# Expert blocks of a mixture of experts: weights as the resting operand in the first two products

## The chip, the cores and the metric

The kernel runs on one core of a Trainium2 chip. The metric is the device time of one execution in microseconds (us). TensorE multiplies matrices: a resting operand of up to 128 x 128 is loaded (LDWEIGHTS, PEld in the profile), and up to 512 columns of a moving operand stream through it (MATMUL, PE). Results land in banks of PSUM, of 128 partitions x 512 float32. VectorE (DVE), ScalarE (ACT) and GpSimd (POOL) work on tiles in SBUF, DVE and ACT also in PSUM; SyncE (SP) issues most transfers.

## What is computed

One layer: an mLSTM mixer, a norm, a mixture of experts, a second norm and a gated embedding, for 1024 tokens of 1024 elements. The change is in the mixture of experts. Each token goes to two of 16 experts:

```python
for e in range(N_EXPERTS):
    h = jax.nn.silu(t @ w_gate[e]) * (t @ w_up[e])
    y = y + gate[:, e:e + 1] * (h @ w_down[e]).astype(jnp.float32)
```

`w_gate` and `w_up` are 1024 x 512 and `w_down` is 512 x 1024 in float32. The kernel computes only the tokens that were routed to an expert.

## The kernel before, in words

To keep float32 accuracy at TensorE's faster rate, each operand is split in a high part (a rounded copy, made by ScalarE) and a low part (the rest, made by VectorE or GpSimd). A product is three matmuls: high x high, high x low, low x high (`product`, line 60, and `split`, line 56).

The experts are worked through in 16 steps, r = 0 to 15. They are ranked by their number of tokens, and `ORDER` (line 42) takes ranks 0, 8, 1, 9 and so on: even r are the eight experts of ranks 0 to 7, odd r the others. Every expert has a first block of 128 tokens. Those of ranks 0 to 7 have a second block of 64 (`mini`, line 716). Tokens beyond these go to a loop at the end that runs as often as the routing asks (line 1461).

For a step r the order is: rows of tokens are gathered (`locate`, 739) and transposed by TensorE (`turn`, 746; `turn_mini`, 750); the gate product; a silu; the up product; their product h; the transposes of h; the down product. In gate and up products the transposed tokens rest and 512 columns of the weights stream. `first_full` (600) does this for 128 tokens: one bank, eight steps of three matmuls. `first_mini` (626) does it for the second block: the 64 high parts and the 64 low parts of its tokens rest side by side, so two matmuls a step do, and `fold` (658) adds the two halves of the bank. h comes out with tokens on partitions and is transposed (`tr_full`, 581, with 128 tokens; `tr_mini`, 592, with 64) for `full_out` (672) and `mini_out` (687).

The main loop (1353) interleaves: while expert r's up and down products run, the gate product of r + 1 stands between them, and the transposes of the tokens of r + 2 stand among the steps of the down product of r (line 1423). The transposes of h of an odd r stand behind the gate product of 128 tokens of r + 1 (line 1400) and ahead of its `first_mini` (1404). Those of an even r stand after four steps of the next gate product (1388).

Weights come in pieces of 1 MB, six to an expert, through four raw buffers (line 486), and each piece is split in two chunks of 1024 columns. The splits wait in a queue (`queue_piece`, 513) and `tick` (542) takes one out after every second step of products; GpSimd makes the low part of every fourth piece. In this stage the order of TensorE, ScalarE, VectorE and GpSimd is the order of the program text (`manual_schedule`, 971 to 976); SyncE's is set by a planner.

PSUM has four banks for products (`pmm`, 491) and three for transposes (`ptr`, 405).

Of the kernel before, what the change touches and what calls it, by code (L numbers as in the profile page):

```python
# [13 lines left out]
F32 = mybir.dt.float32  # L14
# [10 lines left out]
D = 1024  # L25
# [20 lines left out]
def trunk(ctx, tc, io, out):  # L46
# [77 lines left out]
    # ------------------------------------------------ token mixer  # L124
    pw = ExitStack()
    with ExitStack() as pa:
# [34 lines left out]
        def first_load():  # L161
            """the first units' weights and columns of x, in the order of their use"""
# [18 lines left out]
        def qk_units(*us, first=False, between=lambda: None):  # L181
            """the convolved queries or keys of heads; between is traced after half of the products"""
# [75 lines left out]
        def gates():  # L258
            """the gates' running sums and maxima, in two steps"""
# [142 lines left out]
        # output projection's weights and first rows, beside the last of the input projection  # L402
# [62 lines left out]
        def mixed(t, p):  # L465
            """a tile's gated heads and their parts, in steps; the last leaves the transposes"""
# [26 lines left out]
    # ------------------------------------------------ experts' parts  # L493
# [10 lines left out]
    def new_piece(kind):  # L504
        """kind: 0 and 1 for the first products' weights, 2 for the second's"""
# [7 lines left out]
    def queue_piece(raw, shape, kind, eng=None):  # L513
        """a piece whose split is queued, to be traced among the products"""
# [27 lines left out]
    def tick():  # L542
        """after a step of products: every second a queued split, if the clock runs"""
# [6 lines left out]
    def load_part(fetch, m, eng=None, kind=None):  # L550
        """the two pieces of an expert's m-th weights"""
# [9 lines left out]
    def find_tokens(e, parts, nt=NT, p=None, pi=None):  # L561
        """tokens of slots: e [128 tokens, nt, slots] marks a slot's token; parts: ranges of slots"""
# [18 lines left out]
    def tr_full(res, src, nk, name):  # L581
        """[128 tokens, nk * 128] to the parts of its transpose, [128, nk, 128 tokens]"""
        if nk == NF:
            both = mt([128, 2, nk, 128], F32R, name=name)
            res += [both[:, i] for i in range(2)]
        else:
            res += [mt([128, nk, 128], F32R, name=f"{name}{i}") for i in range(2)]
# [22 lines left out]
    def first_halves(res, x, w):  # L610
        """as first_full, the products with the weights' hi parts first, and by halves of the columns"""
# [27 lines left out]
    def part(f, *a):  # L639
        """a list for what a chain makes, and the chain"""  # L640
# [3 lines left out]
    def run(chain, n=NT * NE, also=None, first=0, every=1):  # L644
        """the next n steps of a chain of products, with the steps of another among them"""
# [17 lines left out]
    def silu(g, n):  # L663
        sg = mt([128, DE], F32, name="sg")
# [22 lines left out]
    def mini_out(h, w, dst):  # L687
        yo = mt([128, D], F32, name="yo")
        for n in range(2):
            ps = pmm.tile([128, 512], F32, name="mm")  # L690
            ns = slice(512 * n, 512 * n + 512)
            for k in range(NF):
                wh, wl = use(w[k // 2])
                product(ps, [(h[0][:, k], wh[:, k % 2, ns]), (h[0][:, k], wl[:, k % 2, ns])],
# [21 lines left out]
    mini = lambda i: ORDER[i] < NMINI  # L716

# [11 lines left out]
    def late_fetch(raw, m, half):  # L729
        """a fetch for the second block's expert from the scalar engine's queue"""  # L730
# [3 lines left out]
    def mark(e, v, width):  # L734
        """marks of a position's tokens: e [128 tokens, NT, width]"""
# [3 lines left out]
    def locate(r):  # L739
        """gathers of a block's tokens, by the table's columns"""  # L740
        e = ORDER[r]
        X[r] = gather_x(tab[:, 0, e:e + 1], 128)
        if mini(r):
            XM[r] = gather_x(tab[:, 1, e:e + 1], 64)

    def turn(r):
        rows, X[r] = X[r], []
# [11 lines left out]
    def embed():  # L759
        """rows of the embedding's projection, in steps"""  # L760
# [19 lines left out]
    # ------------------------------------------------ output projection, norm, router  # L780
    pm_, pe_ = ExitStack(), ExitStack()
    with ExitStack() as pb_:
# [10 lines left out]
        # the norm's gain and bias go into the router's weights:  # L793
        # x1 @ rw = (z @ (g rw) - mean sum(g rw)) / std + b @ rw
# [19 lines left out]
        def residual(t):  # L814
            """the residual's rows of a tile"""
# [3 lines left out]
        def project(t, yt):  # L819
            """a tile's output projection in steps"""  # L820
# [17 lines left out]
        def normed(t, n):  # L838
            """half of a tile's sum, its parts and its moments"""
# [49 lines left out]
        def select(c0, c1, new=None):  # L889
            """the experts of tiles c0 to c1: scores and one-hots of the two"""  # L890
# [12 lines left out]
            def places(res, a, m):  # L903
                """of every four in a: how many come before it, larger or as large and to its left"""
# [68 lines left out]
        for t in range(NT - 1):  # L973
# [38 lines left out]
            if t < NT - 2:  # L1012
# [23 lines left out]
             "xgm xt0 xt1 ht sg yo idx idf ohb ef wi svb bs mv")  # L1036
        space = [mt([128, D], F32, name="space", tag=f"xt{i}") for i in range(2)]
# [58 lines left out]
    # ------------------------------------------------ experts  # L1096
    with pe_:
        PIECES[2] = [pe_.enter_context(pool(f"moew{i}", reuse_waits="tile")) for i in range(4, 6)]
        home(pe_.enter_context(pool("moex", reuse_waits="tile")), "xg")
        home(pm_.enter_context(pool("moem", reuse_waits="tile")), "xm hm gs us fold e")  # L1100
# [28 lines left out]
        # what the slots need takes the room of constants that are no longer needed  # L1129
# [7 lines left out]
        key, idr = r1(), r1()  # L1137
# [577 lines left out]
```

## Time and profile before

| | |
|---|---|
| three runs | 1011.25, 1011.89, 1013.51 us |
| median | 1011.89 us |
| span of the profiled execution, first to last instruction | 1008.3 us |
| what lies around that span, against the median | 3.6 us |
| TensorE busy | 973.3 us, 97% |
| VectorE, ScalarE, GpSimd busy | 667.0, 561.8, 302.0 us |
| mean granted clock of TensorE | 0.989 of full speed |

The profile shows one execution. A row of the timeline gives the start and the duration in us, the engine, the line of the kernel, the operation, the tile written and the tiles read, and in brackets the idle time ahead of it with what ended it. A matmul's duration is its way through the pipeline; how fast matmuls follow each other is read from their starts. Line 63 is in `product`, line 57 the high part and 58 the low part of a split, lines 522 and 523 those of a weight piece.

### The profile page before, as it was taken

To read this page: it belongs to the slowest core of one execution; us is meant where nothing else is said; L and a number is where in the kernel's file an instruction comes from. 1 tells how busy PE (TensorE), PEld (TensorE's weight loads), DVE (VectorE), ACT (ScalarE), POOL (GpSimd) and SP (SyncE) were. 2 spreads that over 40 slices of the span, in tenths; PEclk is the share of its full clock that TensorE was granted. 3 is DMA by queue.
4 is the path that set the end of the run, shared out by engine and by line. 5 is a ranking of instruction groups with operands and counts; after the bars stand their busy time and mean duration, and the time that the engine had idled before them with its cause. 6 is when DMAs were issued, how large, how long until landed. Compare 5 with 4: busy or idle time off the path is not lost. (4 is left out here: it accounts for less than half of the span.)

```text
span 1008.3 us, 15211 instructions
## 1 busy us (share of the span) xinstructions
PE 973.3 (97%) x5596; PEld 823.0 (82%) x5596; DVE 667.0 (66%) x1217; ACT 561.8 (56%) x928; POOL 302.0 (30%) x269
## 2 busy tenths in 40 slices
PE   7999999999999999997789999999999999989998
PEld 5989999899999887886467687878787878767887
DVE  6567667461542578879966689866657575577883
ACT  6346546363562455665447666766767676653431
POOL 0002203030100112225647424334252524354442
PEclk9999999999999999999979999999999999999999
DMA  8126811203354364522657998989898988754531
GB/s 320 47 69 266 305 58 59 84 33 93 101 183 155 136 251 150 187 67 117 223 177 289 377 330 290 342 290 335 297 336 298 342 325 296 268 194 149 184 127 63
DMA packets 51396, 207.05 MB, mean 205 GB/s; under 512 B 6892, under 2 KB 15724, under 8 KB 38264
## 3 DMA queue, kind: packets, MB, share of 16 engines
q1 hardware_dynamic: 43720, 182.74, 50.4%
q0 software_dynamic: 5824, 21.50, 6.1%
q10 hardware_dynamic: 1776, 1.81, 0.5%
q8 instruction: 45, 0.74, 0.3%
q14 instruction: 31, 0.25, 0.1%
HBM read 170.35 MB, written 35.68 MB: 204 GB/s over the span
## 5 line engine op out<-in xcount | busy, mean ns | idle before, releaser
L523 POOL TENSOR_TENSOR wlo<-wraw,whi 128x1024 fp32r<-128x1024 f32 x64 | 166.2, 2615 | 223.9 <-ACT whi L522 211.4
L522 ACT ACTIVATE whi<-wraw 128x1024 fp32r<-128x1024 f32 x204 | 205.5, 1051 | 12.9 <-DMA wraw<-eu 4.3
L523 DVE TENSOR_TENSOR wlo<-wraw,whi 128x1024 fp32r<-128x1024 f32 x140 | 172.5, 1259 | 38.8 <-ACT whi L522 37.7
L63 PE MATMUL mm<-whi,xt 128*128 128x512 f32 (+1 forms) x528 | 171.9, 396 | 2.2 <-DVE xt L58 1.5
L63 PE MATMUL mm<-wl,xh 128*128 128x256 f32 (+1 forms) x512 | 145.9, 285 | 0.0
L63 PE MATMUL mm<-wh,xh 128*128 128x256 f32 (+1 forms) x512 | 145.6, 284 | 0.0
L63 PE MATMUL mm<-wh,xl 128*128 128x256 f32 (+1 forms) x512 | 145.4, 284 | 0.0
L63 PEld LDWEIGHTS mm<-whi,xt 128*128 128x128 f32 x528 | 98.6, 191 | 23.7 <-DVE xt L58 2.0
L63 PE MATMUL mm<-wlo,xt 128*128 128x512 f32 (+1 forms) x264 | 100.9, 391 | 4.5 <-DVE wlo L523 4.5
L63 PEld LDWEIGHTS mm<-wh,xh 128*128 128x128 f32 x512 | 97.0, 189 | 0.1
L63 PEld LDWEIGHTS mm<-wl,xh 128*128 128x128 f32 x512 | 96.9, 189 | 0.1
L63 PEld LDWEIGHTS mm<-wh,xl 128*128 128x128 f32 x512 | 96.9, 189 | 0.0
L63 PE MATMUL mm<-woh,yt 128*128 128x512 f32 x256 | 93.6, 412 | 0.0
L63 PE MATMUL mm<-whi,ht 128*128 128x512 f32 x240 | 87.4, 413 | 2.3 <-ACT ht L57 1.4
L63 PE MATMUL mm<-whi,x2t 128*128 128x512 f32 (+1 forms) x272 | 84.7, 386 | 0.4 <-ACT x2t L57 0.4
L63 PEld LDWEIGHTS mm<-wlo,xt 128*128 128x128 f32 x264 | 49.5, 191 | 14.2 <-DVE wlo L523 4.9
L63 PEld LDWEIGHTS mm<-whi,x2t 128*128 128x128 f32 x272 | 50.1, 188 | 11.2 <-ACT x2t L57 0.9
L58 DVE TENSOR_TENSOR wl<-wr,wh 128x1024 fp32r<-128x1024 f32 (+2 forms) x26 | 29.7, 1144 | 44.3 <-ACT wh L57 44.0
L63 PE MATMUL mm<-xh,wh 128*128 128x512 f32 x128 | 50.7, 405 | 7.1 <-ACT xh L57 7.1
L63 PEld LDWEIGHTS mm<-whi,ht 128*128 128x128 f32 x240 | 45.5, 190 | 13.5 <-ACT ht L57 2.0
L63 PEld LDWEIGHTS mm<-woh,yt 128*128 128x128 f32 x256 | 48.1, 188 | 8.8
L63 PE MATMUL mm<-whi,xm 128*128 128x512 f32 x128 | 52.7, 412 | 0.0
(381 smaller groups left out, 2042.2 us busy)
## 6 DMA issues: line engine op xcount, KB each, us to landing
wraw<-eg SPq DMA_DIRECT2D x32, 1024.0 KB, 7.0
wraw<-ed SPq DMA_DIRECT2D x32, 1024.0 KB, 6.3
wraw<-eu SPq DMA_DIRECT2D x31, 1024.0 KB, 6.5
y_d<-zt SPq DMA_DIRECT2D x16, 512.0 KB, 5.6
y_d<-yo SPq DMA_DIRECT2D x14, 512.0 KB, 6.2
num_d<-nb SPq DMA_DIRECT2D x32, 128.0 KB, 1.8
wr<-wo SPq DMA_DIRECT2D x8, 512.0 KB, 4.6
sig_d<-sg SPq DMA_DIRECT2D x32, 128.0 KB, 1.8
```

What stands on the lines that cost most here:

```text
L58: (eng or V).tensor_tensor(lo, src, f32(hi), op=ALU.subtract)
L63: PE.matmul(ps, a, b, start=start and i == 0, stop=stop and i == n - 1)
L522: S.activation(hi[:, c], raw[:, c], AF.Copy)
L523: e.tensor_tensor(lo[:, c], raw[:, c], f32(hi)[:, c], op=ALU.subtract)
```

## The change

For the seven even steps r = 2, 4 ... 14 the gate and up products are turned round: 128 columns of the weights rest, and the tokens of both blocks stream, n = 128 + `extra(r)` of them, high parts and low parts side by side. The weights' high part meets both (2n columns), the low part meets the high parts (n columns). The results have h's columns on partitions, four groups in four banks, so h needs no transposes. `extra` is the size of the second block by rank, 64 for ranks 0 and 1 and 8 fewer for each rank after that. r = 0 stays as it was. The tokens of both blocks are transposed into one tile (`xw`), in four groups instead of two and two, all among the down product of r - 2. Tiles `ht`, `sg`, `xt0` and `xt1` get one buffer instead of two.

```diff
+    def tr_columns(dst, srcs):
+        for src, c0, n in srcs:
+            for q in range(0, ND, 4):
+                turned(src, q, *[dst[:, q:q + 4, i, c0:c0 + n] for i in range(2)], n)
+                yield
+
+    def first_columns(x, w, done):
+        n = x.shape[3]
+        ps = [pmm.tile([128, 512], F32, name="mm") for _ in range(NF)]
+        for half in range(2):
+            for f in range(NF):
+                wh, wl = use(w[half])
+                fs = slice(128 * f, 128 * f + 128)
+                for k in range(4):
+                    xk = x[:, 4 * half + k]
+                    first, end = half + k == 0, half == 1 and k == 3
+                    both = lambda: PE.matmul(ps[f][:, :2 * n], wh[:, k, fs], xk.rearrange("p a c -> p (a c)"),
+                                             start=first, stop=end)
+                    if not end:
+                        both()
+                    PE.matmul(ps[f][:, :n], wl[:, k, fs], xk[:, 0], start=False, stop=False)
+                    if end:
+                        both()
+                if half:
+                    done(f, ps[f])
+                yield
+
+    def gate_columns(n):
+        sg = mt([128, NF, n], F32, name="sgw", bufs=1)
+        def done(f, ps):
+            S.activation(sg[:, f], ps[:, n:2 * n], AF.Copy)
+            V.tensor_tensor(sg[:, f], sg[:, f], ps[:, :n], op=ALU.add)
+            S.activation(sg[:, f], sg[:, f], AF.Silu)
+        return sg, done
+
+    def up_columns(sg):
+        n = sg.shape[2]
+        def done(f, ps):
+            t = mt([128, 192], F32, name="ut", tag=("us", "gs")[f % 2], bufs=1)[:, :n]
+            S.activation(t, ps[:, n:2 * n], AF.Copy)
+            V.tensor_tensor(t, t, ps[:, :n], op=ALU.add)
+            V.tensor_tensor(t, t, sg[:, f], op=ALU.mult)
+            hi = f32(HW[:, f])
+            S.activation(HW[:, f, :n], t, AF.Copy)
+            V.tensor_tensor(HW[:, f, 256:], t[:, :128], hi[:, :128], op=ALU.subtract)
+            G.tensor_tensor(HW[:, f, 192:64 + n], t[:, 128:], hi[:, 128:n], op=ALU.subtract)
+        return done
...
+    turned_too = lambda i: mini(i) and i > 0
+    extra = lambda i: min(64, 72 - 8 * ORDER[i])
...
-            XM[r] = gather_x(tab[:, 1, e:e + 1], 64)
+            XM[r] = gather_x(tab[:, 1, e:e + 1], extra(r))
...
-        V.tensor_scalar(cap, rank, float(NMINI), 64.0, op0=ALU.is_lt, op1=ALU.mult)
+        V.tensor_scalar(cap, rank, -8.0, 72.0, op0=ALU.mult, op1=ALU.add)
+        V.tensor_scalar(one, rank, float(NMINI), None, op0=ALU.is_lt)
+        V.scalar_tensor_tensor(cap, cap, 64.0, one, op0=ALU.min, op1=ALU.mult)
...
+        HW = mt([128, NF, 384], F32R, name="hw", bufs=1)
+        G.memset(f32(HW[:, :, 128:256]), 0.0)
         for r in range(1, NE):
...
             if r < last:
-                u, chain = part(first_full, X[r], WU[r])
+                if mini(r):
+                    chain = first_columns(X[r], WU[r], up_columns(sg))
+                else:
+                    u, chain = part(first_full, X[r], WU[r])
                 run(chain, 2 * (r > 1))
...
-                elif r < last and mini(r + 1):
-                    run(chain, also=turn_mini(r + 1), first=2, every=2)
                 else:
                     run(chain)
-                hf = gated(sg, u[0], 128)
-            if mini(r):
-                sg = silu(gm[0], 64)
-                um, chain = part(first_mini, XM[r], WU[r], "us")
-                run(chain)
-                sg = gated(sg, um[0], 64)
-            if r < last:
+                if mini(r):
+                    ht = HW[:, :, :128], HW[:, :, 256:]
+                    tchain = iter(())
+                else:
+                    hf = gated(sg, u[0], 128)
+                    ht, tchain = part(tr_full, hf, NF, "ht")
                 WU[r + 1] = fetch(r + 1, 1)
-                ht, tchain = part(tr_full, hf, NF, "ht")
...
             if r < last:
-                g, chain = part(first_full, X[r + 1], WG[r + 1])
...
+                if mini(r + 1):
+                    sg, done = gate_columns(X[r + 1].shape[3])
+                    chain = first_columns(X[r + 1], WG[r + 1], done)
+                else:
+                    g, chain = part(first_full, X[r + 1], WG[r + 1])
+                if r == 1:
                     run(chain, 4)
                     clock[1] = 0
-                    run(chain, also=turn_mini(2), every=2)
+                    run(chain)
                     clock[1] = 1
                 else:
                     run(chain)
-                if r + 2 < NE and not mini(r + 1):
+                if r + 2 < NE:
                     WG[r + 2] = fetch(r + 2, 0)
             now(tchain)
-            if r < last:
+            if r < last and not mini(r + 1):
                 sg = silu(g[0], 128)
-            if r < last and mini(r + 1):
-                gm, chain = part(first_mini, XM[r + 1], WG[r + 1], "gs")
-                run(chain)
-                if r + 2 < NE:
-                    WG[r + 2] = fetch(r + 2, 0)
...
             if mini(r):
                 run(chain, 3)
-                hmt, c2 = part(tr_mini, hm, NF, "hm")
-                now(c2)
                 run(chain, also=tx)
...
-                chain = out_mini(r, hmt)
+                chain = out_mini(r, [HW[:, k, 128:256] for k in range(NF)])
```

## Rows read from the trace of the kernel before

**Rows 1.** The page's first part: busy time, share of the span, instructions

```profile
PE 973.3 (97%) x5596; PEld 823.0 (82%) x5596; DVE 667.0 (66%) x1217; ACT 561.8 (56%) x928; POOL 302.0 (30%) x269
```

**Rows 2.** Busy time by stretch: length, five engines, clock, DMA share, GB/s

```profile
780.00:805.00 25.00, 25.00 (x116) 20.49 (x115) 13.97 (x15) 15.82 (x22) 12.77 (x6) 1.00 0.96 352
```

**Rows 3.** Timeline of SP's queue: fetches of gate weights, one pair apart

```profile
702.86 4.95 SPq L725 DMA_DIRECT2D wraw<-eg  x2
...
751.56 4.95 SPq L725 DMA_DIRECT2D wraw<-eg  x2
```

**Rows 4.** Timeline of PE: first matmul of an up product's two parts, and what follows

```profile
697.56 0.39 PE L63 MATMUL mm<-whi,xt 128*128 128x512 f32 x1
...
703.03 0.39 PE L63 MATMUL mm<-whi,xm 128*128 128x512 f32 x1
...
706.77 0.40 PE L63 MATMUL mm<-whi,xt 128*128 128x512 f32 x1
```

**Rows 5.** PE and its weight loads outside the stage; last row from groups by form

```profile
150.36 0.28 PE L63 MATMUL mm<-wh,xh 128*128 128x256 f32 x1
...
151.08 0.28 PE L63 MATMUL mm<-wh,xh 128*128 128x256 f32 x1
...
430.36 0.19 PEld L63 LDWEIGHTS mm<-woh,yt 128*128 128x128 f32 x1
430.47 0.19 PEld L63 LDWEIGHTS mm<-wol,yt 128*128 128x128 f32 x1
...
L63 PE MATMUL pi<-xt,RW 128*32 128x128 f32 x56 | 7.5, 224 | 0.0
```

**Rows 6.** Timeline of PE: four transposes of h and the next matmul

```profile
709.53 0.60 PE L446 MATMUL tr<-cm,sg 128*128 128x128 f32 x4
709.89 0.48 PE L63 MATMUL mm<-whi,xt 128*128 128x512 f32 x1
```

**Rows 7.** Timelines of PE, ACT and DVE: an odd step's h, from transposes to down product

```profile
686.91 0.60 PE L446 MATMUL tr<-cm,sg 128*128 128x128 f32 x4
...
691.09 0.39 PE L63 MATMUL mm<-whi,ht 128*128 128x512 f32 x1
...
687.55 0.60 ACT L57 ACTIVATE ht<-tr 128x512 fp32r<-128x512 f32 x1 [1.66 <-PE tr L446]
...
688.18 0.69 DVE L58 TENSOR_TENSOR ht<-tr,ht 128x512 fp32r<-128x512 f32 x1 [1.95 <-ACT ht L57]
```

**Rows 8.** Timelines of ACT, DVE and POOL: splits in an up product of an even step

```profile
698.25 4.84 ACT L522 ACTIVATE whi<-wraw 128x1024 fp32r<-128x1024 f32 x5
...
699.34 3.50 DVE L523 TENSOR_TENSOR wlo<-wraw,whi 128x1024 fp32r<-128x1024 f32 x3
...
702.28 5.17 POOL L523 TENSOR_TENSOR wlo<-wraw,whi 128x1024 fp32r<-128x1024 f32 x2 [9.15 <-ACT whi L522]
```

**Rows 9.** Timelines of POOL, DVE, ACT and PE around r = 2, then stretches

```profile
557.31 4.76 POOL L523 TENSOR_TENSOR wlo<-wraw,whi 128x1024 fp32r<-128x1024 f32 x2 [3.68 <-ACT whi L522]
...
560.07 2.55 DVE L669 TENSOR_TENSOR sg<-sg,us 64x512 f32<-64x512 f32 x1
...
561.22 2.01 ACT L522 ACTIVATE whi<-wraw 128x1024 fp32r<-128x1024 f32 x2 [1.90 <-DMA wraw<-eu]
563.25 0.60 ACT L57 ACTIVATE ht<-tr 128x512 fp32r<-128x512 f32 x1
...
563.89 0.50 PE L63 MATMUL mm<-whi,ht 128*128 128x512 f32 x1 [1.43 <-ACT ht L57]
...
565.54 0.96 PE L63 MATMUL mm<-whi,ht 128*128 128x512 f32 x2 [0.91 <-DVE ht L58]
...
566.00:568.00 2.00, 2.00 (x6) 1.53 (x5) 1.54 (x2) 2.00 (x4) 0.00 (x0) 0.50 1.00 418
568.00:570.00 2.00, 2.00 (x9) 1.16 (x8) 1.88 (x2) 1.30 (x2) 0.00 (x0) 0.68 1.01 422
```

**Rows 10.** The page's DMA issues: count, KB each, us to landing

```profile
wraw<-eg SPq DMA_DIRECT2D x32, 1024.0 KB, 7.0
```

More of the change, by code (lines that the diff above doesn't have):

```diff
@@ L583, in tr_full @@
         if nk == NF:
-            both = mt([128, 2, nk, 128], F32R, name=name)
+            both = mt([128, 2, nk, 128], F32R, name=name, bufs=1)
             res += [both[:, i] for i in range(2)]
         else:
-            res += [mt([128, nk, 128], F32R, name=f"{name}{i}") for i in range(2)]
+            res += [mt([128, nk, 128], F32R, name=f"{name}{i}", bufs=1) for i in range(2)]
         for q in range(0, nk, 4):
@@ L663, in silu @@
     def silu(g, n):
-        sg = mt([128, DE], F32, name="sg")
+        sg = mt([128, DE], F32, name="sg", bufs=1)
         S.activation(sg[:n], g[:n], AF.Silu)
@@ L693, in mini_out @@
                 wh, wl = use(w[k // 2])
-                product(ps, [(h[0][:, k], wh[:, k % 2, ns]), (h[0][:, k], wl[:, k % 2, ns])],
+                product(ps, [(h[k], wh[:, k % 2, ns]), (h[k], wl[:, k % 2, ns])],
                         k == 0, k == NF - 1)
@@ L743, in locate @@
         if mini(r):
-            XM[r] = gather_x(tab[:, 1, e:e + 1], 64)
+            XM[r] = gather_x(tab[:, 1, e:e + 1], extra(r))
     def turn(r):
-        rows, X[r] = X[r], []
+        rows = X[r]
+        if turned_too(r):
+            n = extra(r)
+            X[r] = mt([128, ND, 2, 128 + n], F32R, name="xw", bufs=1)
+            return tr_columns(X[r], ((rows, 0, 128), (XM[r], 128, n)))
+        X[r] = []
         return tr_full(X[r], rows, ND, "xt")
@@ L1035, in trunk @@
         home(pe_.enter_context(pool("moe", side="right", reuse_waits="tile")),
-             "xgm xt0 xt1 ht sg yo idx idf ohb ef wi svb bs mv")
-        space = [mt([128, D], F32, name="space", tag=f"xt{i}") for i in range(2)]
+             "xgm xt0 xt1 xw ht sg yo idx idf ohb ef wi svb bs mv")
+        both = mt([128, 2, D], F32, name="space", tag="xw", bufs=1)
+        space = [both[:, i] for i in range(2)]
         for k in range(2):
@@ L1135, in trunk @@
         pref = prefs.rearrange("p e c -> p c e")
-        key, idr = r1(), r1()
+        key, idr, one = r1(), r1(), r1()
         big = carve(NE, NE)
@@ L1219, in trunk @@
         va, rk = carve(2, NT), carve(2, NT)
-        one = r1()
         V.tensor_scalar(one, rank, float(ORDER[1]), None, op0=ALU.is_equal)
@@ L1348, in slots @@
             yield
-        chain = out_mini(0, hmt)
+        chain = out_mini(0, [hmt[0][:, k] for k in range(NF)])
         run(chain)
         WD[1] = load_part(FETCH[1], 2, [G, V])
+        HW = mt([128, NF, 384], F32R, name="hw", bufs=1)
+        G.memset(f32(HW[:, :, 128:256]), 0.0)
         for r in range(1, NE):
@@ L1384, in trunk @@
             if r < last:
-                g, chain = part(first_full, X[r + 1], WG[r + 1])
-                if mini(r):
-                    run(chain, 4)
-                    now(tchain)
-                    hm = sg
-                    run(chain)
-                elif r == 1:
+                if mini(r + 1):
[4 more added lines that the diff above has]
+                if r == 1:
                     run(chain, 4)
                     clock[1] = 0
-                    run(chain, also=turn_mini(2), every=2)
+                    run(chain)
                     clock[1] = 1
@@ L1397, in trunk @@
                     run(chain)
-                if r + 2 < NE and not mini(r + 1):
+                if r + 2 < NE:
                     WG[r + 2] = fetch(r + 2, 0)
             now(tchain)
-            if r < last:
+            if r < last and not mini(r + 1):
                 sg = silu(g[0], 128)
-            if r < last and mini(r + 1):
-                gm, chain = part(first_mini, XM[r + 1], WG[r + 1], "gs")
-                run(chain)
-                if r + 2 < NE:
-                    WG[r + 2] = fetch(r + 2, 0)
             if r == 9:
@@ L1567, in turn2 @@
             if i == 0:
-                XT[t] = [mt([128, ND, 128], F32R, name=f"x2t{j}", tag=f"xt{j}") for j in range(2)]
+                if t % 2:
+                    both = mt([128, 2, ND, 128], F32R, name="x2t", tag="xw", bufs=1)
+                    XT[t] = [both[:, j] for j in range(2)]
+                else:
+                    XT[t] = [mt([128, ND, 128], F32R, name=f"x2t{j}", tag=f"xt{j}", bufs=1) for j in range(2)]
             turned(Z[t][0], 4 * i, *[a[:, 4 * i:4 * i + 4] for a in XT[t]])
```

16 lines of the change are left out of this document (8 added, 8 removed).

## The prediction

> **What bounds the kernel now.** I read the page's first part, then busy time by stretch, then the timeline of each engine through one pair of expert blocks, then the rows of TensorE by form. TensorE is busy for 97% of the span [rows 1], and in the expert stage it has no idle time at all while the other engines do; the DMA engines are 96% busy in that stretch and not everywhere so full [rows 2]. The schedule repeats after two blocks, one with a second block of tokens (even r, "E") and one without (odd r, "O"): two fetches of gate weights that stand one pair apart are issued 48.7 us apart [rows 3]. So time taken from TensorE here is time won, as long as nothing makes it wait. The profiled execution's span is 1008.3 us; the median of the runs is 1011.9, 3.6 more, which I add to every span.
>
> **What goes: columns.** A gate or up product of an E block is 24 matmuls of 512 columns for the first block, 5.47 us, and 16 for the second, 3.74 us [rows 4]: 9.21 us. Seven blocks (r = 2, 4 ... 14) have two each: 14 products, 128.9 us. Afterwards a product is 32 pairs: weights' high part against 2n columns, low part against n, with n = 192, 184 ... 144, mean 168. The trace has 256 columns at 0.12 us apart (six steps in 0.72) [rows 5] and 512 at 0.228 [rows 4]; on the line between, the mean 336 columns cost 0.154. Below 256 columns with full weights there is no row. Lower bound: time falls with columns, 0.12 x 168/256 = 0.079; narrow streaming itself isn't punished, since the duration of a matmul of 128 columns is 0.22 us against 0.28 at 256 [rows 5]. Upper bound: the 0.12 of 256. Two weight loads that nothing else holds start 0.11 apart [rows 5], and each narrow matmul must cover the next load, so I take 0.11, close to the upper end. 448 pairs x 0.264 = 118.3 us: **10.6 us won** (6.1 to 24.5).
>
> The Trainium skill ("TensorE: Matmul & The Clock Gate", Back-to-back issue gap) gives N/2.4 + 2.5 ns for a matmul alone: as an estimate 72 ns for 168 columns, by which the sum would win some 17 us more. The load rows speak against it; it is a rival below.
>
> **What goes: transposes.** In E blocks the four transposes of h and the four of the second block's h fall away. Four take 0.36 us of TensorE [rows 6]; the narrower four are taken the same: 14 x 0.36 = **5.0 us won**. The transposes of x are as many as before, moved into the down product of two blocks earlier; their count costs nothing new. Two small vector instructions join the capacity, where DVE waits for other work; the memset of 128 columns goes to POOL: nothing, under cover of POOL's splits. Gathers shrink a little, no queue gains an instruction. Together TensorE has **15.6 us less** to do.
>
> **What comes: O blocks lose a cover.** In an O block the transposes of h stand at the end of the next block's gate product for 128 tokens (686.91); while ScalarE copies them (0.60, done at 688.15) and VectorE makes the low part (0.69, done at 688.87), TensorE runs the 16 matmuls of the second block's gate, and the down product begins at 691.09 [rows 7]. After the change gate products come in one piece, and the transposes stand behind it, directly ahead of the down product that reads them. All four banks drain at the end of that piece. Splits are paced by steps of products, one for two steps: a pair had 72 steps and has 56 for its 24 splits, so four splits no longer run in the first 8 of 16 steps but over all 8, the last behind the last drain. In ScalarE's program order drains and that split stand ahead of the copy of h. Walk, with 0 at the end of the gate product and n = 168: a step is 4 pairs, 1.06 us. An operation of 168 columns costs about 0.35 on ScalarE (between 0.60 for 512 [rows 7] and 4.84/5 = 0.97 for 1024 [rows 8]) and 0.37 on VectorE (0.69 [rows 7] and 3.50/3 = 1.17 [rows 8]). Copy, add and silu of a group follow each other: 1.07. Group 1 is there at -2.1 and done at -1.0, a split until 0, group 2 until 1.1, group 3 until 2.1, the last split until 3.1, h's high part at 3.7. TensorE has its transposes by 0.36 and waits 3.35 us; the low part comes 0.69 later, of which two matmuls cover 0.46. That is 3.6 us. If ScalarE were free, 0.60 + 0.69 - 0.46 = 0.83 would be left: the low end. At r = 1 no splits run, so 2 us there: 6 x 3.6 + 2 = **about 23 us lost** (6 to 25). Late next are the copies of the down product and the turned x, queued behind on ScalarE.
>
> **E blocks.** The up product's four groups each need copy, add, product, copy in line, 1.44 us. The product reads two tiles of SBUF, and such an operation has waited for POOL's split: 2.55 us where one of its size takes 0.69 [rows 7], beside two splits of 4.76 us [rows 9]. POOL's split in an E block (5.17 for two [rows 8]) falls exactly there now. ScalarE, blocked in order, walks to 6.3 us behind the up product's end where before its five splits were done in 4.84 [rows 8]; four more splits, a silu and three copies bring the first copy of turned x to about 13.5. TensorE wants the bank back for the fourth group of transposes (three banks; two groups stood here before, four now) at 5.5 + 2.8 + 3 x 1.06 = 11.5. So 0 to 4 us per E block with a block to turn (r = 2 to 12, six); I take 1.5, nearer to 0, since each earlier hand-over can hide a part: **9 us lost** (0 to 24). A raw buffer that POOL frees later starts its fetch later, and a fetch lands after 7 us [rows 10]; this is inside the upper end.
>
> **Clock.** The trace has such a stall: at r = 2 two splits stood ahead of h's copy on ScalarE, TensorE waited 1.43 and 0.91 us, and then the granted clock was 0.50 in 566 to 568 and 0.68 in 568 to 570 [rows 9], which is the 1.2 GHz level for part of it; (0.50 + 0.32) x 2 = 1.6 us lost. Of the seven longer stalls I let half do that: **6 us** (0 to 21 with all thirteen).
>
> **Sum**: -10.6 - 5.0 + 23 + 9 + 6 = +22.4: span 1030.7, time **1034.3 us**.
>
> **Rivals.** (A) *The saving comes through.* If ScalarE has its queue empty at the ends of the gate products, the O stall is the 0.83 and E blocks lose nothing: -15.6 + 6 = -9.6, 1002.3 us. It decides where less than 15.6/7 = 2.2 us is lost per pair. For it: ScalarE was idle for 1.66 us ahead of the copy of h [rows 7], and it and VectorE are busy some 60% [rows 2]. Against: the order on ScalarE is written out, and the cover is gone in any case; the DMA share of 0.96 [rows 2] leaves little room for a much shorter pair. 0.19.
> (B) *Narrow matmuls stream freely*, loads hidden: 448 x 0.031 = 13.9 us more won. With the stalls 1020.4 (0.12); with A 988 (0.03). Against: 0.11 between loads [rows 5].
> (C) *E blocks pay in full*: 24 instead of 9 and six more of half clock: 1055 us, 0.12. For it the walk's 13.5 against 11.5; against, the longer pair gives ScalarE room.
> (D) *The smaller capacity overflows*: then the loop over extra blocks runs. The reference's router gives sorted loads 168, 163, 163, 148, 138, 134, 131, 126 and less, the expert of 134 being first; capacities are 192, 192, 184, 176, 168, 160, 152, 144, so none does. An extra block would cost at least 72 matmuls, 16.4 us. Under 0.01, inside the slower cases.
>
> **How the numbers follow.** Forecast 0.50 (1022 to 1048), A 0.19, B 0.12 and 0.03, C 0.12, and 0.04 where gain and loss meet within 0.2% (about what a measurement of this kernel can tell from no change). Slower: 0.50 + 0.12 + 0.12 = 0.74; same 0.04; faster 0.19 + 0.03 = 0.22. The range takes in A's centre and C's: 1002 to 1056.
>
> **What would show it.** Right: in O blocks idle time of TensorE ahead of the first down matmul, ended by ScalarE's copy of h, some 3 us, seven times; the transposes of turned x waiting for a bank in E blocks; drops of the granted clock behind these; wide matmuls 0.13 to 0.17 apart, narrow ones 0.11. Wrong: a TensorE without idle time in the stage and pairs of about 46 us (then A), narrow matmuls under 0.10 apart (then B), or waits at other places, of the banks ahead of a gate or up product above all.

## The result and the profile after

The changed kernel takes **1058.78 us** (median of 4 runs, 1057.98 to 1061.42) beside 1011.57 for the kernel before on the same chip: ratio 1.0467, interval 1.045 to 1.0485. Slower, as forecast; but 47 us slower and not 22, and 2.8 us above the top of the range. The profiled executions are 1056.2 and 1008.3 us long, 47.9 apart, and every reading below compares these two.

First the page's first part, to be read beside [rows 1]:

```profile
PE 979.8 (93%) x5876; PEld 846.5 (80%) x5876; DVE 681.9 (65%) x1289; ACT 567.9 (54%) x998; POOL 313.0 (30%) x298
```

TensorE has less to do, and yet it is busy for 6.5 us more: a sign that part of its work ran at the lower clock. Next, what TensorE waits for (us in total, times, the longest):

```profile
PE mm L63 <- ACT ht L57: 18.2, 7, 2.8
PE tr L446 <- DVE xw L58: 12.5, 4, 3.2
PE mm L63 <- POOL wlo L523: 6.9, 7, 2.3
...
PE tr L446 <- DVE trips L1378: 3.3, 1, 3.3
...
PE mm L619 <- DVE sg L726: 2.9, 1, 2.9
```

Before, of all these there were only 1.4 and 0.9 us for h at r = 2. The first line is the O blocks' wait for h. The second and the fourth are the fourth group of transposes of turned x in E blocks, five times (in one of them the last thing that VectorE did was a small operation of the router, L1378). The third is a low part of w_down that GpSimd makes. The last is a bank for the gate product, once.

One O block in the timeline (start, duration). TensorE, h's transposes and the down product behind them:

```profile
657.62 0.60 PE L446 MATMUL tr<-cm,sg 128*128 128x128 f32 x4
661.05 0.50 PE L63 MATMUL mm<-whi,ht 128*128 128x512 f32 x1 [2.83 <-ACT ht L57]
```

ScalarE in the same time, in its order:

```profile
658.52 0.30 ACT L635 ACTIVATE sgw<-mm 128x176 f32<-128x176 f32 x1
659.22 0.35 ACT L637 ACTIVATE sgw<-sgw 128x176 f32<-128x176 f32 x1 [0.40 <-DVE sgw L636]
659.48 1.04 ACT L522 ACTIVATE whi<-wraw 128x1024 fp32r<-128x1024 f32 x1
660.42 0.58 ACT L57 ACTIVATE ht<-tr 128x512 fp32r<-128x512 f32 x1
```

The gate product ends at 657.62, the last drain (a group's results read out of its bank) at 659.57; the split stands behind it, and only then comes the copy of h, done at 661.00. That is 3.4 us behind the end of the product, where the walk of the prediction had 3.7 (in [rows 7] the down product followed h's transposes after 16 other matmuls).

One E block in the timeline. ScalarE, from the splits behind the drains to the copy of turned x:

```profile
683.79 4.83 ACT L522 ACTIVATE whi<-wraw 128x1024 fp32r<-128x1024 f32 x5
...
691.39 1.08 ACT L57 ACTIVATE xw<-tr 128x512 fp32r<-128x512 f32 x2
```

VectorE, from a drain to the low part of turned x:

```profile
679.68 0.34 DVE L648 TENSOR_TENSOR ut<-ut,mm 128x176 f32<-128x176 f32 x1 [0.86 <-ACT ut L647]
680.05 2.12 DVE L649 TENSOR_TENSOR ut<-ut,sgw 128x176 f32<-128x176 f32 x1
...
685.82 3.70 DVE L523 TENSOR_TENSOR wlo<-wraw,whi 128x1024 fp32r<-128x1024 f32 x2 [0.98 <-ACT whi L522]
...
689.51 2.35 DVE L523 TENSOR_TENSOR wlo<-wraw,whi 128x1024 fp32r<-128x1024 f32 x2
691.78 0.15 DVE L1405 TENSOR_SCALAR trb<-trb 128x8 f32<-128x8 f32 x1
691.86 2.35 DVE L523 TENSOR_TENSOR wlo<-wraw,whi 128x1024 fp32r<-128x1024 f32 x2
694.13 0.68 DVE L58 TENSOR_TENSOR xw<-tr,xw 128x512 fp32r<-128x512 f32 x1
```

GpSimd, a split beside that drain:

```profile
679.58 2.39 POOL L523 TENSOR_TENSOR wlo<-wraw,whi 128x1024 fp32r<-128x1024 f32 x1 [0.61 <-ACT whi L522]
```

TensorE, its two waits in the down product:

```profile
687.35 0.50 PE L63 MATMUL mm<-wlo,hw 128*128 128x512 f32 x1 [1.23 <-POOL wlo L523]
...
694.86 0.44 PE L446 MATMUL tr<-cm,xgm 40*128 40x40 f32 x4 [3.24 <-DVE xw L58]
```

The up product ends at 678.19. ScalarE's first copy of turned x starts 13.2 us later, at 691.39 (the walk: 13.5). But a bank is free only when VectorE has made its low part too, and VectorE starts that at 694.13, behind six low parts of weights. The first two of these took 3.70 us beside another split of GpSimd's (684.92 to 687.30), where the next two took 2.35. TensorE waits until 694.86.

Busy time by stretch behind the two waits (a line closes with the granted clock, the DMA share and GB/s; behind the stretch stand its length and TensorE's busy time):

```profile
660.00:664.00 4.00, 2.95 (x8) 2.09 (x9) 2.93 (x4) 1.95 (x3) 3.40 (x3) 0.77 0.09 12
664.00:670.00 6.00, 6.00 (x30) 4.93 (x30) 3.00 (x6) 3.83 (x6) 1.05 (x2) 0.87 0.91 305
694.00:698.00 4.00, 3.14 (x13) 2.54 (x14) 2.47 (x7) 1.84 (x3) 2.60 (x2) 0.78 0.97 393
698.00:702.00 4.00, 4.00 (x15) 3.17 (x14) 0.69 (x2) 1.10 (x3) 3.22 (x2) 0.79 0.81 267
```

Behind either wait the clock is at its lower level, 1.2 GHz, for part of the next stretches, just when TensorE works again. That is 1.7 us of clock lost behind each (4 x 0.22 + 4 x 0.21 for the second). The same reading behind the other waits: it is 1.7 us as well behind two more for h (six us from 603 and from 719 read 0.72) and behind two more of the fourth group (from 637 and from 808, 0.72). Behind three waits for h of 2.8 us the clock does not fall (the first three lines), nor behind the one of 1.25 us at r = 1. Two waits of the fourth group and the one for the bank cost 3.4 us each (the last three lines):

```profile
775.00:781.00 6.00, 4.71 (x21) 3.60 (x22) 2.77 (x2) 3.53 (x5) 5.17 (x4) 1.00 0.31 87
830.00:836.00 6.00, 5.38 (x27) 4.14 (x27) 3.21 (x3) 3.52 (x7) 5.00 (x3) 1.00 0.46 147
884.00:890.00 6.00, 4.55 (x21) 3.45 (x22) 2.77 (x2) 3.53 (x5) 3.09 (x2) 1.00 0.28 72
...
750.00:758.00 8.00, 6.46 (x18) 5.15 (x19) 2.74 (x6) 2.80 (x6) 5.21 (x3) 0.57 0.96 369
859.00:867.00 8.00, 5.59 (x16) 4.49 (x17) 3.31 (x6) 2.96 (x6) 4.52 (x2) 0.57 1.00 363
588.00:598.00 10.00, 7.12 (x33) 6.90 (x32) 6.26 (x9) 2.09 (x5) 1.48 (x1) 0.66 0.95 356
```

So the waits for h brought 5.1 us of lost clock (three of seven), those of the fourth group 11.9 (five of five), the bank 3.4. In sum: the mean granted clock of the span is 0.969, and 1056.2 x 0.031 = 32.7 us are missing; before 1008.3 x 0.011 = 11.1. That is 21.6 us more.

Last, the products, here the start of one of n = 176 (wide and narrow matmuls in turn):

```profile
648.89 0.32 PE L619 MATMUL mm<-xw,whi 128*128 128x352 f32 x1
649.05 0.24 PE L623 MATMUL mm<-xw,wlo 128*128 128x176 f32 x1
649.13 0.35 PE L619 MATMUL mm<-xw,whi 128*128 128x352 f32 x1
649.32 0.24 PE L623 MATMUL mm<-xw,wlo 128*128 128x176 f32 x1
649.40 0.35 PE L619 MATMUL mm<-xw,whi 128*128 128x352 f32 x1
```

The whole product runs from 648.89 to the transposes at 657.62: 8.73 us. The one at n = 192 takes 9.12, the last, at n = 144, runs from 892.29 to 900.14, 7.85. Over the 14 it is 118.9 us (for the one in which the bank was waited for, the 8.93 of its neighbour of the same n).

| term | forecast, us | measured, us |
|---|---|---|
| products | -10.6 | -10.0 (128.9 to 118.9) |
| transposes of h | -5.0 | -5.0 (14 groups at 0.36 gone) |
| O blocks, wait for h | +23 | +15.9 (18.2 less 2.3 before) |
| E blocks, turned x, w_down's low part, bank | +9 | +25.6 (15.8 + 6.9 + 2.9) |
| clock | +6 | +21.6 |
| sum | +22.4 | +48.1 of 47.9 |

Smaller waits elsewhere rose and fell by 1 to 2 us each and about cancel.

### The profile page after: what moved, and what is told of

It is laid out like the page before. It is cut to its first block, busy times and chain, and to the rows that moved or that the text cites. A ratio compares the mean times of both kernels' runs of the same rounds, so it can differ in the third digit from the quotient of the medians.

```text
span 1056.2 us, 15916 instructions
## 1 busy us (share of the span) xinstructions
PE 979.8 (93%) x5876; PEld 846.5 (80%) x5876; DVE 681.9 (65%) x1289; ACT 567.9 (54%) x998; POOL 313.0 (30%) x298
## 4 chain that ended last, share of the span: by engine, by line
PE 39%; DVE 14%; ACT 7%; issue 3%; POOL 2%; DMA 1%; DVEq 0%; ACTq 0%; POOLq 0%
PE mm L63 28%; PE mm L619 5%; DVE wlo L523 4%; ACT whi L522 4%; PE mm L623 2%; PE tr L446 2%; DVE ut L649 2%; POOL wlo L523 2%; PE tr L459 1%; DMA wraw<-pgw 1%; DVE sgw L636 1%; DVE ut L648 1%; ACT hw L651 1%; DVE shift L923 1%; ACT sgw L637 1%
## 5 line engine op out<-in xcount | busy, mean ns | idle before, releaser
L523 DVE TENSOR_TENSOR wlo<-wraw,whi 128x1024 fp32r<-128x1024 f32 x140 | 184.8, 1361 | 46.7 <-ACT whi L522 46.2
L619 PE MATMUL mm<-xw,whi 128*128 128x384 f32 (+6 forms) x448 | 122.4, 351 | 2.9 <-DVE sg L726 2.9
L623 PE MATMUL mm<-xw,wlo 128*128 128x192 f32 (+6 forms) x448 | 101.6, 247 | 0.0
L63 PE MATMUL mm<-whi,xt 128*128 128x512 f32 (+1 forms) x304 | 95.3, 389 | 5.5 <-DVE xt L58 3.4
L619 PEld LDWEIGHTS mm<-xw,whi 128*128 128x128 f32 x448 | 82.7, 192 | 3.7 <-DVE sg L726 3.1
L623 PEld LDWEIGHTS mm<-xw,wlo 128*128 128x128 f32 x448 | 85.0, 194 | 0.6
L63 PE MATMUL mm<-whi,hw 128*128 128x512 f32 x168 | 70.0, 447 | 0.0
L63 PEld LDWEIGHTS mm<-whi,xt 128*128 128x128 f32 x304 | 56.0, 191 | 17.2 <-DVE xt L58 3.7
L63 PE MATMUL mm<-whi,ht 128*128 128x512 f32 x128 | 49.9, 446 | 18.2 <-ACT ht L57 18.2
L63 PE MATMUL mm<-wlo,xt 128*128 128x512 f32 (+1 forms) x152 | 57.8, 400 | 2.6 <-DVE wlo L523 2.6
```

Of the source, the lines that this page charges most:

```text
L63: PE.matmul(ps, a, b, start=start and i == 0, stop=stop and i == n - 1)
L523: e.tensor_tensor(lo[:, c], raw[:, c], f32(hi)[:, c], op=ALU.subtract)
L619: both = lambda: PE.matmul(ps[f][:, :2 * n], wh[:, k, fs], xk.rearrange("p a c -> p (a c)"), start=first, stop=end)
L623: PE.matmul(ps[f][:, :n], wl[:, k, fs], xk[:, 0], start=False, stop=False)
```

## The experiments

Each kernel is the changed one with the edit shown; where no interval is given, the time is that of one run, beside one of the kernel before on the same chip. The waits are compared with those of the change, above.

**Give the O blocks their cover back.**

```diff
                 else:
+                    if mini(r + 1):
+                        run(chain, 4)
+                        now(tchain)
                     run(chain)
```

(At r = 1 the same, behind the four steps that stand there.)

> Edit: in odd blocks the transposes of h stand after four of the eight steps of the next block's gate product (turned form), no longer behind it; nothing else moves. Theory (h's copy queues on ScalarE behind four drains and a split because nothing stands between transposes and down product): the seven waits of TensorE for h, 18.2 us after the change, fall under 2 us, the half-clock stretches that begin right behind them (at 604, 662 and 720 us among others) go too, worth 1.7 us each; time 1030 to 1040 us. Rival (ScalarE, VectorE or the transfers as a whole are too slow for the shorter pair): the waits come back elsewhere, on splits or raw buffers, and the time stays above 1050 us.

1045.1 us, beside 1011.34. What TensorE waits for:

```profile
PE mm L63 <- POOL wlo L523: 14.1, 8, 2.3
PE tr L446 <- DVE xw L58: 11.0, 4, 3.2
PE mm L63 <- DVE wlo L523: 6.2, 4, 4.5
```

The waits for h are gone, all seven. But GpSimd's low parts, not sooner than before, now end waits of 7.2 us more (of VectorE's 6.2 us, 4.5 stand at 505 us, ahead of these blocks, where the kernel before has the same), and the mean clock is 0.968, as low as ever. Behind the E blocks' five waits the lost clock is 11.9 us as in the change; behind three of GpSimd's longer waits (1.8 to 2.3 us, ending at 574, 843 and 895) it is 5.1, what the O blocks' waits had brought. So the mechanism holds, and the gain of 14 us is less than the theory's 19 to 29. The rival is right in part.

**Two groups of turned x back in the O block.**

```diff
+                elif not mini(r):
+                    run(chain, also=tx, every=2)
                 else:
                     run(chain)
...
                 run(chain, 3)
-                run(chain, also=tx)
+                run(chain, also=islice(tx, 2))
```

> Edit: of the four groups of transposes of the next turned x only two stand in an even block's down product; the second block's two go back into the odd block's up product, as in the kernel before. Theory (the fourth group waits for a bank whose reader is late): the 15.8 us of TensorE's waits ahead of transposes of x (12.5 and 3.3) fall under 3 us, with most of the half clock that follows them; time 1035 to 1045 us. Rival 1 (ScalarE's backlog itself is late, not the fourth group): the wait moves to the next thing that ScalarE owes, the copy of the down product or of h, and the time stays above 1050. Rival 2: the groups in the odd block's up product wait for ScalarE there: 1045 to 1055.

1034.85 us, beside 1011.34. The 15.8 us ahead of transposes are gone entirely, the 18.2 for h are 19.1, and the missing clock is 24.8 us (0.976 of 1032.8) where it was 32.7. Waits and clock together make 15.8 + 7.9 - 0.9 = 22.8 of the 23.4 us that the span lost. The theory, just under its range; neither rival.

**Splits out of the drains' way.**

```diff
+    def run_columns(chain, n=4):
+        for _ in zip(range(n), chain):
+            tick()
+            tick()
...
                 else:
+                    if mini(r + 1):
+                        run_columns(chain)
+                        now(chain)
                     run(chain)
```

(The same in the up product of E blocks, two steps ahead of the gathers and two behind.)

> Edit: in the turned gate and up products the four weight splits stand one behind each of the first four steps, none behind the last four; in the change they stand behind every second step. Theory (order on ScalarE): no split stands among the drains, so h's copy and the first copies of turned x come one to two splits (1.0 to 2.0 us) sooner: the waits for h fall from 2.6 us each to about 1 to 1.6, the waits ahead of the fourth group from 3.1 to 1 to 2; time 1035 to 1048 us. Rival (the waits come of the drains' own length, or the splits then wait for their transfers and hold ScalarE up): waits unchanged or new waits of ScalarE for raw buffers; 1054 us or more.

1033.94 us, beside 1011.34, 1 us better than the best of the theory. The same number of splits, only earlier:

```profile
PE mm L63 <- ACT ht L57: 8.7, 7, 1.5
PE tr L446 <- DVE xw L58: 8.6, 4, 2.4
...
PE mm L63 <- POOL wlo L523: 3.6, 2, 2.3
```

All three waits shrink at once, h's to half, and the missing clock to 24.8 us. So the order on ScalarE, and of the low parts that follow it, sets these waits, not the amount of work; GpSimd's low part was late because its split was.

**GpSimd's low parts to VectorE.**

```diff
-        eng = eng or (G if pieces[0] % 4 == 0 else V)
+        eng = eng or V
```

> Edit: the low parts that GpSimd makes in the expert stage (one piece in four) go to VectorE; GpSimd keeps its small part of h. Theory (GpSimd's splits hold VectorE's two-input operations and are late themselves): TensorE's seven waits for GpSimd's low part of the down weights (6.9 us) go, VectorE's product in the up drains takes 0.4 us and no longer 2.1, and the waits of the fourth group shrink by 1 us or more each; time 1040 to 1050 us. Rival (VectorE has too much to do then, 6 splits of 1.17 us more for a pair): h's low part and VectorE's splits are late instead; 1058 us or more.

1054.27 us, beside 1011.34: 4 us won, hardly more than the 3.4 by which the change's own runs differ, and 4 to 14 missed. The seven waits for GpSimd are gone, and all four products of an E block take 0.34 us, such as

```profile
679.49 0.34 DVE L649 TENSOR_TENSOR ut<-ut,sgw 128x176 f32<-128x176 f32 x1
```

where one took 2.12. But h's waits rise to 23.8, with 2.6 for its low part, and the transposes still wait 12.7. VectorE pays what GpSimd no longer does: theory and rival are both true, and about cancel.

**The first two together, then all three.**

> Edit: the first and the second edit together (h's transposes after four steps of the gate product; two groups of turned x back in the odd block's up product). Alone they gave 1045.1 and 1034.85 us, where the change has 1058.8, and the first alone left as much half clock as the change has. Theory (the waits are each their own, and half clock comes behind any of them as long as one is left in a pair): both sums of waits, 18 and 16 us, go, only GpSimd's low part of the down weights is left to wait for (7 to 14 us), and now half clock goes too; time 1008 to 1020 us. Rival (gains of the two overlap, since each wait gives ScalarE time to catch up): GpSimd's and VectorE's low parts and the raw buffers become the wait; 1025 us or more.

1017.48 us, beside 1009.88: in the theory's range. No wait for h or for a transpose; 14.2 us for GpSimd's low parts are left, the missing clock is 19.3 us (0.981 of 1015.4).

> Edit: the first three edits together (h's transposes after four steps, two groups of turned x in the odd block's up product, the turned products' splits behind their first four steps). Theory (the change is 15.6 us less work with waits added; with the waits gone the saving shows): GpSimd's low parts are made sooner as well, waits in the expert stage under 6 us in sum, half clock as in the kernel before; time 996 to 1006 us, under the 1011.3 of the kernel before. Rival (the pair is bound by ScalarE, GpSimd or transfers at about the length it had): 1008 to 1025 us, with waits of TensorE for weight pieces or of splits for raw buffers.

1003.75 us, beside 1009.88: the theory. Busy time from 600 to 850 us, with the columns of above, first in the kernel before:

```profile
600.00:850.00 250.00, 250.00 (x1170) 201.25 (x1169) 173.42 (x202) 173.11 (x228) 92.58 (x44) 1.00 0.87 314
```

In the change:

```profile
600.00:850.00 250.00, 219.87 (x1193) 187.84 (x1192) 162.36 (x227) 150.39 (x240) 88.86 (x60) 0.95 0.74 267
```

With the three edits:

```profile
600.00:850.00 250.00, 248.69 (x1463) 218.75 (x1463) 193.67 (x264) 181.50 (x291) 104.56 (x69) 1.00 0.89 331
```

TensorE has no idle time before, 30.1 us in the change, at a lower clock besides, and 1.3 us here. Of the waits that are left from r = 1 on, 7.8 us stand between 540 and 594 us, at r = 1 to 3.

**Work for nothing in the waits.** This one prices the clock: 16 matmuls ahead of an O block's down product, 18 ahead of the fourth group, into a bank that nothing reads.

```diff
+    def fillers(n, a):
+        pi = pix.tile([128, 512], F32, name="pi")
+        for _ in range(n):
+            PE.matmul(pi[:, :a.shape[1]], a[:, :128], a, start=True, stop=True)
...
             now(tchain)
+            if r < last and mini(r + 1):
+                fillers(16, X[r + 1][:, 0].rearrange("p a c -> p (a c)"))
...
-                run(chain, also=tx)
+                run(chain, 4, also=islice(tx, 3))
+                if r + 2 < NE and turned_too(r + 2):
+                    fillers(18, HW[:, 0])
+                now(tx)
+                run(chain)
```

> Edit: the kernel of the change, with matmuls that nothing reads put into a spare bank where TensorE waits: 16 of 2n columns between an odd block's transposes of h and its down product, 18 of 384 columns ahead of the fourth group of turned x. The output is the same; the waits stay as long as they were, but TensorE streams in them. Theory (half clock comes behind TensorE's idle stretches, and costs 20 us): the ends of the products stay where they were relative to each other except for the half clock; granted clock 1.00 through nearly all of the stage, time 1038 to 1048 us. Rival 1 (half clock is not brought by these stretches): clock as in the change and time 1055 to 1062. Rival 2 (the half clock slows TensorE where it would have waited anyway, so that it costs nothing): clock 1.00 and waits longer by as much, 1055 or more.

1048.35 us, beside 1009.88, with a span of 1046.6. More work, and 9.6 us less than the change. The same stretch:

```profile
600.00:850.00 250.00, 243.94 (x1406) 213.24 (x1405) 170.06 (x235) 160.40 (x255) 92.08 (x62) 1.00 0.75 279
```

The clock is 1.00 in it, where the change has 0.95. The fillers take 41.1 us (13 stretches of 2.9 to 3.4), and they stand in for 34.0 - 2.6 = 31.4 us of waits, 2.6 being left for h; so they lengthen the path by 9.7. Without that the gain would have been 9.6 + 9.7 = 19.3 us, and the clock's own account is 32.7 - 15.7 = 17.0, as much as the 5.1 and 11.9 us that were read behind these waits above. The theory's 20 us is right to a few us; both rivals fall.

**The best of them, timed.** The three edits again, then with splits in the gate product of r = 1 too, then with 64 places for every rank.

> The kernel with the three edits together again, now timed: one look gave 1003.75 us beside 1009.88 of the kernel before. Theory (the saving of the change shows once the waits are gone): 0.991 to 0.995 of the kernel before. Rival (the one look was a lucky one, or another chip's): within 0.2% of the kernel before.

Median 1007.1 us of 12 runs (1003.13 to 1012.8) beside 1010.32 of 23 (1007.45 to 1014.04): ratio 0.9978, interval 0.9957 to 0.9999. Just faster; between theory and rival, and the single run above stood at the good end.

The splits at r = 1:

```diff
-                if r == 1:
-                    run(chain, 4)
-                    clock[1] = 0
-                    now(tchain)
-                    run(chain)
-                    clock[1] = 1
-                else:
...
+                if mini(r + 1):
+                    run_columns(chain)
+                    now(tchain)
+                    now(chain)
+                run(chain)
```

> Edit on top of the three: the splits run in the gate product of r = 1 too (steps and splits stopped there in the change, as in the kernel before). The three edits together leave waits of TensorE for splits and low parts at r = 1 and 2 (some 9 us between 540 and 594) and half clock behind them. Theory (a backlog of splits from r = 1 is carried into r = 2): 4 to 8 us less than the three edits, 996 to 1000 us. Rival (the splits there wait for their transfers and hold ScalarE's drains up): no gain or 2 us lost, 1003 to 1006.

Median 1001.3 us of 6 (998.03 to 1007.3): ratio to the kernel before **0.992**, interval 0.9889 to 0.995, and 5.8 us under the three edits, within the 4 to 8 of the theory. This kernel beats both. The page's first part:

```profile
PE 956.8 (96%) x5876; PEld 835.1 (84%) x5876; DVE 687.6 (69%) x1289; ACT 565.2 (57%) x998; POOL 311.6 (31%) x298
```

TensorE is busy for 956.8 us beside 973.3 [rows 1]: 16.5 less, near the 15.6 that the prediction worked out. So the saving was real; the change gave it back in waits. Of the 16.5 us the repaired kernel shows 12.4 in its span (995.9 beside 1008.3) and 9.0 in the medians; TensorE is idle for 4.1 us more than before.

The capacity, on top of the three edits:

```diff
-    extra = lambda i: min(64, 72 - 8 * ORDER[i])
+    extra = lambda i: 64
...
-        V.tensor_scalar(cap, rank, -8.0, 72.0, op0=ALU.mult, op1=ALU.add)
+        V.tensor_scalar(cap, rank, 0.0, 64.0, op0=ALU.mult, op1=ALU.add)
```

> Edit on top of the three: 64 places in the second block for every rank, 384 and 192 columns instead of 384 to 288 and 192 to 144. In the change's trace a product takes 9.12 to 9.22 us at 192 tokens and 7.85 at 144. Theory (TensorE's columns are on the path in every even block): 2 x (0.2 + 0.4 + 0.65 + 0.9 + 1.15 + 1.3) = 9 us more, 1011 to 1014, most of the change's saving being the capacity by rank. Rival (pairs are paced by something else by now): under 3 us more.

Median 1012.04 us of 12 (1004.97 to 1015.59), ratio to the kernel before 1.0001 (0.9979 to 1.0023), 4.9 us above the three edits. In its trace every undisturbed up product takes 9.12 us, and the 14 products together 7.7 us more than with the capacity by rank; the two profiled spans are 9.1 apart. The medians give half of that, with runs that scatter by 10 us; so the columns are on the path, and the exact size stays open between 5 and 9. That is most of the saving of the products: at 192 tokens a product takes 9.12 us where the old form took 9.21, so of the 10.0 us the form alone gives 14 x 0.09 = 1.3, and the rest comes of streaming fewer columns for the smaller ranks.

**Who holds the fourth group: ScalarE or VectorE?** `force` is a list that holds None until the edit sets it.

```diff
-            e.tensor_tensor(lo[:, c], raw[:, c], f32(hi)[:, c], op=ALU.subtract)
+            (force[0] or e).tensor_tensor(lo[:, c], raw[:, c], f32(hi)[:, c], op=ALU.subtract)
...
+                force[0] = G if r > 2 else None
                 run(chain, 3)
                 run(chain, also=tx)
+                force[0] = None
```

> Edit: the kernel of the change, but the weight splits of the first block's down product in even blocks from r = 4 on leave their low parts to GpSimd, so that VectorE has two of 1.17 us fewer ahead of the low parts of the turned x. ScalarE's order stays. In the change the fourth group of transposes waits until 694.75 us in one such block, where ScalarE copied the group before at 691.39 and VectorE took it up only at 694.13, behind its low parts of weights. Theory (VectorE's queue ends the wait, not ScalarE's): the waits ahead of that group fall from 3.2 us each to 0.5 to 1.5, in sum from 15.8 to under 8, and the time to 1042 to 1053 us. Rival 1 (ScalarE's copies end it): unchanged within 0.5 us each. Rival 2 (GpSimd's longer work holds VectorE's two-input operations, which then are late all the same): waits as long or longer, and later ones for GpSimd's low parts; 1058 or more.

1063.26 us, beside 1012.08, the slowest of all: the second rival, but for GpSimd's low parts, which end waits of 6.9 us as before. VectorE in one E block:

```profile
688.52 4.52 DVE L523 TENSOR_TENSOR wlo<-wraw,whi 128x1024 fp32r<-128x1024 f32 x2
692.97 2.30 DVE L1405 TENSOR_SCALAR trb<-trb 128x8 f32<-128x8 f32 x1
695.18 0.68 DVE L58 TENSOR_TENSOR xw<-tr,xw 128x512 fp32r<-128x512 f32 x1
```

ScalarE's copy in the same block:

```profile
690.40 1.07 ACT L57 ACTIVATE xw<-tr 128x512 fp32r<-128x512 f32 x2
```

TensorE's waits ahead of the transposes:

```profile
PE tr L446 <- DVE xw L58: 14.3, 4, 5.3
```

GpSimd's three splits run from 689.20 to 697.56. Beside them two low parts take 4.52 us and not 2.35, and an operation of 8 columns takes 2.30 and not 0.15. ScalarE copies turned x at 690.40, as early as ever, and the wait grows to 5.3 us with VectorE's start at 695.18. So VectorE's queue ends this wait; and work taken off it is no help if GpSimd does it at the same time. What a shorter queue of VectorE's alone would give, this run does not show.

## Why the prediction was wrong in size

**The sign, and why, was right.** Products and transposes came out within 0.6 us. The sum of a pair of matmuls was right, 0.265 us where the sum had 0.264, but by luck, since its two parts were not: the wide one takes 0.19 and the narrow one 0.08 at n = 176, forecast as 0.154 and 0.11. At n = 144 a pair still takes 0.245. By the prediction's own sign (narrow matmuls under 0.10 apart) rival B would have come; it is excluded by the pair's sum, which shows none of the 13.9 us more that B would win. The Trainium skill's formula for a matmul alone ("TensorE: Matmul & The Clock Gate", Back-to-back issue gap) would give, as an estimate, 0.076 + 0.149 us for such a pair; the trace agrees for the narrow one and not for the wide one, and the measurement decides.

**O blocks: +23, measured +15.9.** The mechanism is the one forecast and shown by undoing it. The walk was long by 0.3 us, the low part of h (put down for 0.2) cost nothing more, and TensorE's own transposes ended 0.6 us behind the product and not 0.36: together 2.8 in place of 3.6 each. The 2.3 us of waits that the kernel before had at r = 2, and that went, were not in the sum.

**E blocks: +9, measured +25.6. Here a step failed.** "TensorE wants the bank back for the fourth group", walked as ScalarE's 13.5 against 11.5: ScalarE's walk was right to 0.3 us, but the bank has a second reader. The walk ended at ScalarE's copy and never carried VectorE's queue on, where six low parts of weights, two of them stretched beside GpSimd's split, stand ahead of the turned x: VectorE was done at 694.81, 16.6 us behind the up product and not 13.5. TensorE came late too, 13.4 us behind it and not 11.5, 1.2 of that from its own wait for GpSimd's low part; so the wait was 3.2 us. And the 1.5 was chosen "nearer to 0, since each earlier hand-over can hide a part". Next to nothing was hidden: five blocks paid 3.1 to 3.3 us each; only the sixth, r = 2, paid nothing here, after 2.3 for GpSimd's low part a little earlier. The low part of w_down (6.9 us) was not in the walk at all, and the bank ahead of a gate product (2.9), which the prediction named as a sign of being wrong, came once.

**Clock: +6, measured +21.6.** The price of one stall came from [rows 9], 1.6 us, and most stretches of half clock cost that, 1.7 us. "Of the seven longer stalls I let half do that" came nearly true: three of the seven did, 5.1 us. The step that failed is again the E blocks, whose waits were let bring nothing: all five did, two of them at double the price, 11.9 us, and the bank 3.4. The upper end, "21 with all thirteen", fits the 21.6 by luck: nine waits brought 20.4 of it, three of them at 3.4.

**The rivals.** A (the saving comes through) failed in the change and is what the repaired kernel does. C (E blocks in full, with their half clock; 1055) was the nearest, and had 0.12; its mechanism, with VectorE as the last reader, should have been the forecast. The range missed by 2.8 us because its upper end took C's centre and nothing beyond it.

## What to carry to other kernels

A product that runs in one piece where there were two also has fewer steps on which other work is paced (here 8 where there were 16); look whose copies then queue behind the last drains, and hang the paced work on the first steps rather than on all. Follow a buffer to its last reader, through that engine's queue, before a wait is priced. Where TensorE is the bound, 41.5 us of waits cost half as much again in clock, so small waits in each pair undid a saving of 15 us four times over.

## What the runs showed of the hardware that I had not expected

- An operation of VectorE on 8 columns of SBUF took 2.30 us beside GpSimd's splits and 0.15 elsewhere, and the product of two SBUF tiles 2.12 and 0.34; sums that read PSUM (L648) took 0.34 right beside it. The Trainium skill ("SBUF — State Buffer", SBUF: two separate sides) has it that VectorE and GpSimd share a pair of ports which one of them holds for a whole instruction: the trace agrees.
- Behind waits of 2.8 us in O blocks the clock fell three times of six in the change, and six times of six when the E blocks' waits were gone (the second edit: 0.72 over the six us from 601, 656, 707, 758, 809 and 860). Behind those of the E blocks it fell five times of five in the change and in the first edit, for 1.7 us or for 3.4. Which wait brings a drop is thus not simply a matter of its length; why, no run here shows.
- At n = 176 a narrow matmul starts 0.19 us behind the wide one, and the next wide one 0.08 behind the narrow. A pair takes 9.12/32 = 0.285 us at 192 tokens and 7.85/32 = 0.245 at 144: a quarter fewer columns, 14% less time. What takes the rest, weight loads or something else, no run here shows.
